# Layer 0's feed-forward in seven block products, with its down-projection a stage of its own, and the state-space tables in two parts

## The chip, the cores and the metric

The kernel runs on one core of a Trainium2 chip. The time is the device time of one execution in microseconds (us). The engines are named as in the profile: PE (TensorE, matrix products, with PEld its weight loads), DVE (VectorE), ACT (ScalarE), POOL (GpSimd) and SP (SyncE, which here issues the DMAs). Each engine works through its own instructions in the order in which the program holds them, and waits where one of them needs another engine's result.

## What is computed

Two layers over 1024 positions of width 1024, all in fp32. Layer 0's mixer is latent attention beside a short gated convolution; layer 1's is a complex-diagonal state-space model. Behind each mixer stands a feed-forward with a convolution of width 3 over the positions; its hidden width is 2816.

```
def conv_ffn(h, w_up, conv_w, w_down):
    up = causal_depthwise_conv(h @ w_up, conv_w)
    gate, val = jnp.split(up, 2, axis=-1)
    return (jax.nn.silu(gate) * val) @ w_down

for layer in range(DEPTH):
    x = x + (mla_shortconv_mixer if layer % 2 == 0 else s5_mixer)(rms_norm(x, ...), ...)
    x = x + conv_ffn(rms_norm(x, ffn_norm[layer]), ffn_w_up[layer], ffn_conv_w[layer], ffn_w_down[layer])
```

The state-space mixer needs, from its small parameters alone, tables for its 64 groups of 16 channels and 64 states: powers of the complex decay, input and output matrices, and a short convolution kernel. They depend on no activation.

## The kernel before

The activations lie transposed in eight tiles xT[0] to xT[7], 128 channels by 1024 positions. Every fp32 product is made of three fp32r products of a high and a low part (`PASSES`: high x high, high x low, low x high), so a product of a 1024-deep unit with 128 columns, `mm_unit` (L175), is 8 x 3 x 2 = 48 matmuls of 128x128 by 128x512. `split_w` (L153, L154) makes the two parts of a weight tile, the high one on ACT, the low one on POOL. Engines run what a scheduler has put in their streams; it orders instructions by the place where the code makes them, as far as their inputs allow.

**Short convolution** (functions up to L290). For m = 0 to 3 there are three units, c, i and b. DVE evicts each from PSUM times the norm (`scaled`, L268: uc, ui, ub), makes the product ut = uc x ui (L282), two steps of the convolution (cv, L285 and L287) and cv x ub (L290); POOL makes the low part cgl (L294). Two down-projections (`down`, L190 matmuls, L193 evictions into xT) follow m = 3. Then comes attention, and behind it the last part of the mixer's down-projection, `down(last_at, w_last, after=bd, skip=3)`.

**Layer 0's feed-forward** (`ffn`). 44 units of 48 matmuls, a gate and a value unit for each of 22 rows; DVE evicts and convolves (L757 to L764), multiplies (L808), and after each pair of rows `down` adds the pair's part of the down-projection, 96 matmuls. Beside it run the state-space tables, in steps: `param_steps` advances the generator `Params.stages` by one, and `ffn` calls it at several places of each row pair.

**The tables** (`Params`). `base` is a chain of some 160 small DVE operations of 128x32 (L868 to L881: exponentials, sine and cosine by polynomials, squarings). `powers` makes the powers of the decay. A `unit(q)`, 16 of them, has three steps: (a) a transpose on PE (pct), and eight small operations (L1042 to L1047, cm and sr); (b) twelve outer products on DVE (L1055 to L1060, tiles z, 128x256 and 128x288); (c) four transposes (pet, L1112) and four small products (pk, L1123) on PE, evictions on ACT and DMAs that store the results in memory. At last 16 `turns(q)`, each a set of outer products of 128x256.

**Layer 1's feed-forward** is done in seven block products: the up-projection's depth of 1024 is cut into two halves of 512, the positions into two halves, and the four block products of a row pair are replaced by seven products of sums of blocks (`Pair`, products "1" to "7", L1648, 12 matmuls each; 22 pairs, 154 products). The sums of the inputs are made in `NormBoundary.second_half`, the sums of weights in `Pair.sums` (POOL, L1628) and `Pair.weights`. The gated rows go to memory (gfd) and the down-projection is a stage of its own behind it, in groups of two and then four rows (`rows`, L1796 the low parts). The inputs xT are stored in memory before they are overwritten and loaded again for the down-projection.

Of the kernel before, what the change touches and what calls it, by code (L numbers as in the profile page):

```python
# [11 lines left out]
F32 = mybir.dt.float32  # L12
# [38 lines left out]
def hybrid_trunk_kernel(ctx: ExitStack, tc: tile.TileContext, xt, gains, mix_w_in, w_uq, w_ukv, q_gain, k_gain,  # L51
# [193 lines left out]

    bases = {"c": CB + CC, "i": CB + 2 * CC, "b": CB}
    with phase("pa") as pA:
# [12 lines left out]
        rx = bd.r  # L260
    pbs = ctx.enter_context(ExitStack())
# [9 lines left out]
    for gr in range(2):  # L271
        gts = []
        for i in range(2):
            m = 2 * gr + i
            if m:
# [3 lines left out]
            ui = scaled(ps_i, "ui")  # L279
            t = pB.tile([P, S + 2], F32, tag="ut", name="ut")  # L280
# [7 lines left out]
                                           op0=ALU.mult, op1=ALU.add)  # L288
            ub = scaled(mm_unit(split_w(ws[2]), xa) if m else first_ps[2], "ub")
# [13 lines left out]
    pbs.close()  # L303
    pR0.close()
# [3 lines left out]
    with phase("pc") as pC, tc.tile_pool(name="psa", bufs=1, space=PSUM, reuse_waits="tile") as pa:  # L308
# [374 lines left out]
        if True:  # L683
# [39 lines left out]
            up_raw = []  # L723
            for n in range(2):
                queue[1].turn()
                up_raw.append(load_up(0, n))
# [5 lines left out]
            up_raw.append(load_up(0, 2))  # L732
            retire(queue.pop(0))()
            add_row()
            up_first = [split_w(r) for r in up_raw]
            tc_order.close()
        last_at = [groups[gr].at for gr in (2, 3)]
        w_last = [w_rows[gr] for gr in (2, 3)]
# [8 lines left out]
    def ffn(layer, bd, rbpool, open_pool, gtile, down_last, background=lambda: None, first=None):  # L747
        dn = ffn_w_down[layer]

        def convolve(ps, m, gate):  # L750
            res = []
            for hf in range(2):
                u = pF.tile([P, HALF + 2], F32, tag="u", bufs=2, name="u")
                if hf == 0:
                    nc.vector.memset(u[:, 0:2], 0.0)
                else:
                    nc.vector.tensor_copy(out=u[:, 0:2], in_=u_last[:, HALF:HALF + 2])  # L757
                u_last = u
                nc.vector.tensor_tensor(out=u[:, 2:HALF + 2], in0=ps[hf], in1=rb[:, HALVES[hf]], op=ALU.mult)  # L759
                c = pF.tile([P, HALF], F32, tag="c", bufs=4, name="c")  # L760
                nc.scalar.activation(c, u[:, 2:HALF + 2], AF.Copy, scale=cwcol(layer, 2, m))  # L761
                nc.vector.scalar_tensor_tensor(out=c, in0=u[:, 1:HALF + 1], scalar=cwcol(layer, 1, m), in1=c,
                                               op0=ALU.mult, op1=ALU.add)
                nc.vector.scalar_tensor_tensor(out=c, in0=u[:, 0:HALF], scalar=cwcol(layer, 0, m), in1=c,  # L764
                                               op0=ALU.mult, op1=ALU.add)
                if gate:
                    nc.scalar.activation(c, c, AF.Silu)
                res.append(c)
            return res

        xs = bd.xs
        prev = None
        loads = [lambda m=m: load_up(layer, m) for m in range(3, 2 * NM)]
        ps, rb = first_units(first or [split_w(load_up(layer, m)) for m in range(3)], xs, bd, rbpool)
        pF = open_pool()
        raw, ready = [loads.pop(0)()], []

        def unit():

            res = ps.pop(0) if ps else mm_unit(ready.pop(0), xs)  # L780
            if len(ps) <= 1:
                if raw:
                    ready.append(split_w(raw.pop(0)))
                if loads:
                    raw.append(loads.pop(0)())
            return res

        def rows_of(gr):
            return [load_row(dn, 2 * gr + i) for i in range(2)]

        for gr in range(NG):
            gts = []
            for i in range(2):
                m = 2 * gr + i
                if gr > 1:
                    background()
                cg = convolve(unit(), m, True)
                if gr:
                    background()
                if gr and i:  # L800
                    rows = [split_w(r) for r in rows]
                cv = convolve(unit(), NM + m, False)
                if gr and not i:
                    rows = rows_of(gr - 1)
                gh, gl = gtile(pF, "gh"), gtile(pF, "gl")
                for hf in range(2):
                    cols = HALVES[hf]
                    nc.vector.tensor_tensor(out=cv[hf], in0=cv[hf], in1=cg[hf], op=ALU.mult)  # L808
                    nc.scalar.activation(gh[:, cols], cv[hf], AF.Copy)  # L809
                    nc.gpsimd.tensor_tensor(out=gl[:, cols], in0=cv[hf], in1=gh[:, cols].bitcast(F32),  # L810
                                            op=ALU.subtract)
# [1061 lines left out]
```

## Time and profile before

| | us |
|---|---|
| median of three runs (lowest, highest) | 2345.22 (2342.04, 2348.31) |
| the profiled execution, and its span | 2344.66, 2342.9 |
| short convolution, to the last matmul of its down-projections | 49.4 to 196.38 |
| attention | 201.76 to 513.86 |
| last part of the mixer's down-projection | 513.86 to 530.91 |
| layer 0's feed-forward with the tables | 530.91 to 1293.39 |
| state-space mixer and its output | 1293.39 to 1628.08 |
| layer 1's products | 1644.60 to 2096.77 |
| layer 1's down-projection | 2096.77 to 2337.94 |

The dates come from the chain of work that ended last: starting at the last instruction, it names at each step what released it, or the instruction before it on its engine. The stretch view gives, for the time between two dates, how long each engine was busy and with how many instructions, the granted TensorE clock (1.00 is full speed) and the mean busy share of the DMA engines. TensorE was busy for 2248.5 us of the span.

### The profile page before, as it was taken

To read this page: it belongs to the slowest core of one execution; us is meant where nothing else is said; L and a number is where in the kernel's file an instruction comes from. 1 tells how busy PE (TensorE), PEld (TensorE's weight loads), DVE (VectorE), ACT (ScalarE), POOL (GpSimd) and SP (SyncE) were. 2 spreads that over 40 slices of the span, in tenths; PEclk is the share of its full clock that TensorE was granted. 3 is DMA by queue.
4 is the path that set the end of the run, shared out by engine and by line. 5 is a ranking of instruction groups with operands and counts; after the bars stand their busy time and mean duration, and the time that the engine had idled before them with its cause. 6 is when DMAs were issued, how large, how long until landed. Compare 5 with 4: busy or idle time off the path is not lost.

```text
span 2342.9 us, 29810 instructions
## 1 busy us (share of the span) xinstructions
PE 2248.5 (96%) x11228; PEld 1867.9 (80%) x11228; DVE 1614.7 (69%) x2650; ACT 851.3 (36%) x1446; POOL 767.0 (33%) x575
## 2 busy tenths in 40 slices
PE   7999899999999999999999988999789999999999
PEld 6888888888788878888888877788568888878887
DVE  6344677787978778879777487323888888876542
ACT  4112566664232333332223255312444444443110
POOL 4322454435233222232224344431043333324220
PEclk9999999999999999999999998999999999999999
DMA  4112000012122221223332288521132222245301
GB/s 155 45 38 57 1 10 10 10 46 72 29 66 62 82 68 49 76 80 92 101 102 63 93 223 242 171 72 41 54 110 93 82 81 81 81 153 181 125 10 72
DMA packets 227152, 192.04 MB, mean 82 GB/s; under 512 B 25472, under 2 KB 202944, under 8 KB 227008
## 3 DMA queue, kind: packets, MB, share of 16 engines
q1 hardware_dynamic: 227008, 190.14, 26.9%
q8 instruction: 88, 1.44, 0.2%
q14 instruction: 56, 0.46, 0.1%
HBM read 148.22 MB, written 46.07 MB: 83 GB/s over the span
## 4 chain that ended last, share of the span: by engine, by line
PE 79%; DVE 11%; issue 3%; DMA 3%; ACT 3%; POOL 1%; SPq 0%; DVEq 0%; POOLq 0%; ACTq 0%
PE pu L175 31%; PE pd L190 22%; PE pc L1648 4%; PE pb L1648 4%; PE pa L1648 4%; PE pd L1648 2%; PE pu L1554 1%; PE pss L586 1%; PE po L634 1%; PE pckv L378 1%; PE pq L446 1%; PE ptp L615 1%; DVE xT L1696 1%; PE pcq L378 1%; PE pda L644 1%
## 5 line engine op out<-in xcount | busy, mean ns | idle before, releaser
L154 POOL TENSOR_TENSOR wl<-raw,wh 128x1024 fp32r<-128x1024 f32 (+2 forms) x115 | 289.1, 2515 | 487.3 <-ACT wh L153 242.3
L193 DVE TENSOR_TENSOR xT<-pd,xT 128x512 f32<-128x512 f32 x320 | 204.3, 682 | 160.4 <-PE pd L190 159.8
L153 ACT ACTIVATE wh<-raw 128x1024 fp32r<-128x1024 f32 (+2 forms) x117 | 122.4, 1051 | 305.8 <-PE pu L175 212.6
L175 PE MATMUL pu<-f_h,wh 128*128 128x512 f32 x704 | 219.4, 393 | 0.0
L175 PE MATMUL pu<-f_l,wh 128*128 128x512 f32 x704 | 217.2, 390 | 0.0
L175 PE MATMUL pu<-f_h,wl 128*128 128x512 f32 x704 | 216.7, 389 | 0.0
L175 PEld LDWEIGHTS pu<-f_l,wh 128*128 128x128 f32 x704 | 132.1, 188 | 27.9
L175 PEld LDWEIGHTS pu<-f_h,wl 128*128 128x128 f32 x704 | 132.1, 188 | 27.9
L175 PEld LDWEIGHTS pu<-f_h,wh 128*128 128x128 f32 x704 | 130.7, 188 | 28.7 <-issue 1.7
L810 POOL TENSOR_TENSOR gl<-c,gh 128x512 fp32r<-128x512 f32 x44 | 61.4, 1415 | 247.0 <-ACT gh L809 247.0
L1696 DVE SCALAR_TENSOR_TENSOR xT<-u,vec,xT 128x1024 f32<-128x1024 f32 x84 | 111.1, 1330 | 13.3 <-ACT xT L1694 12.6
L759 DVE TENSOR_TENSOR u<-pu,f_rb 128x512 f32<-128x512 f32 x88 | 56.8, 685 | 89.9 <-PE pu L175 87.9
L190 PE MATMUL pd<-gh,wh 128*128 128x512 f32 x352 | 113.5, 403 | 5.4 <-DVE u L759 2.9
L190 PE MATMUL pd<-gh,dwh 128*128 128x512 f32 x352 | 108.8, 390 | 2.5 <-DVE xT L193 1.5
L190 PE MATMUL pd<-gl,wh 128*128 128x512 f32 x352 | 110.4, 395 | 0.0
L190 PE MATMUL pd<-gh,wl 128*128 128x512 f32 x352 | 110.0, 394 | 0.0
L190 PE MATMUL pd<-gh,dwl 128*128 128x512 f32 x352 | 108.5, 389 | 0.0
L190 PE MATMUL pd<-gl,dwh 128*128 128x512 f32 x352 | 108.4, 389 | 0.0
L1796 POOL TENSOR_TENSOR dwl<-raw,dwh 128x1024 fp32r<-128x1024 f32 x20 | 60.8, 3066 | 112.5 <-PE pd L190 84.3
L761 ACT ACTIVATE c<-u,vec 128x512 f32<-128x512 f32 x88 | 59.9, 717 | 69.5 <-DVE u L759 69.1
L190 PEld LDWEIGHTS pd<-gh,wh 128*128 128x128 f32 x352 | 65.8, 191 | 22.6 <-DVE xT L193 4.0
L190 PEld LDWEIGHTS pd<-gh,dwh 128*128 128x128 f32 x352 | 66.1, 188 | 16.9 <-DVE xT L193 1.9
(569 smaller groups left out, 5790.6 us busy)
## 6 DMA issues: line engine op xcount, KB each, us to landing
raw<-in_ffn_w_up_dram SPq DMA_DIRECT2D x50, 512.0 KB, 3.8
raw<-in_ffn_w_down_dram SPq DMA_DIRECT2D x42, 512.0 KB, 4.4
xT<-in_ffn_w_up_dram SPq DMA_DIRECT2D x40, 512.0 KB, 3.6
gfd<-xT SPq DMA_DIRECT2D x21, 512.0 KB, 2.6
raw<-gfd SPq DMA_DIRECT2D x20, 512.0 KB, 4.0
raw<-in_w_glu_dram SPq DMA_DIRECT2D x16, 512.0 KB, 4.0
raw<-in_mix_w_in_dram SPq DMA_DIRECT2D x14, 512.0 KB, 3.9
xT<-in_xt_dram SPq DMA_DIRECT2D x8, 512.0 KB, 7.6
```

Source lines behind the costliest of these rows:

```text
L153: nc.scalar.activation(h[:, 0:n], raw[:, 0:n], AF.Copy)
L154: eng.tensor_tensor(out=l[:, 0:n], in0=raw[:, 0:n], in1=h[:, 0:n].bitcast(F32), op=ALU.subtract)
L175: nc.tensor.matmul(ps[hf], lhsT=w[wi][:, P * k:P * k + P], rhs=xs[k][xi][:, HALVES[hf]], start=(k == 0 and wi == 0 and xi == 0), stop=(k = ...
L190: nc.tensor.matmul(ps[hf], lhsT=ws[i][wi][:, P * f:P * f + P], rhs=gts[i][xi][:, HALVES[hf]], start=(i == first and wi == 0 and xi == 0), ...
L193: nc.vector.tensor_tensor(out=xT[f][:, HALVES[hf]], in0=ps[hf], in1=xT[f][:, HALVES[hf]], op=ALU.add)
L378: nc.tensor.matmul(ps[:, HALF * j:HALF * j + n], lhsT=xa[k][xi][:, P * (2 * p + j):P * (2 * p + j) + P], rhs=w[k // kw][wi][:, n * (k % kw ...
L759: nc.vector.tensor_tensor(out=u[:, 2:HALF + 2], in0=ps[hf], in1=rb[:, HALVES[hf]], op=ALU.mult)
L761: nc.scalar.activation(c, u[:, 2:HALF + 2], AF.Copy, scale=cwcol(layer, 2, m))
L810: nc.gpsimd.tensor_tensor(out=gl[:, cols], in0=cv[hf], in1=gh[:, cols].bitcast(F32), op=ALU.subtract)
L1648: nc.tensor.matmul(ps, lhsT=w[:, HALF * wi + P * k:HALF * wi + P * k + P], rhs=x.at(xi, k), start=(start and k == 0 and wi == 0 and xi == ...
L1696: nc.vector.scalar_tensor_tensor(out=c, in0=u[:, w:S + w], scalar=cwcol(self.layer, w, m), in1=c, op0=ALU.mult, op1=ALU.add)
L1796: eng.tensor_tensor(out=l, in0=raw, in1=h.bitcast(F32), op=ALU.subtract)
```

## The change

Layer 0's feed-forward is done as layer 1's is. The code of layer 1 becomes the class `FeedForward(layer)` with the methods `add`, `sums`, `spread`, `first_half`, `second_half`, `up`, `rows` and `begin_down`, and `Pair(ff, m)`; layer 1 uses it with unchanged steps. From the state-space stage on every engine holds the same instructions in the same order as before. The last part of the mixer's down-projection is made half by half of the positions; the first half's norm is begun during the second half.

The class `Params` moves ahead of the first stage and its generator is cut in two. `first_part` has base, powers and units 0 to 7, is driven by calls in the short convolution (two steps a call, three calls for each m) and by every second block of its two down-projections, and then stores what the rest needs (`keep`, 128x1314) in memory. `second_part` loads it again, has units 8 to 15 and the turns, and is driven by one step for each of the eight blocks f of each group of layer 0's new down-projection. The loads and splits of the first three units of layer 0's up-projection at the end of attention are gone.

```diff
@@ short convolution, for each m = 2 * gr + i
             ui = scaled(ps_i, "ui")
+            background(2)
             t = pB.tile([P, S + 2], F32, tag="ut", name="ut")
...
+            background(2)
             ub = scaled(mm_unit(split_w(ws[2]), xa) if m else first_ps[2], "ub")
...
             gts.append((gh, gl))
+            background(2)
...
-            down(*held_down)
-            down(gts, wr)
+            down(*held_down, after=lambda f: background(f % 2))
+            down(gts, wr, after=lambda f: background(f % 2))
@@ Params
+        def first_part(self):
+            yield from self.base()
...
+            yield from self.units(0, SPLIT)
+            nc.sync.dma_start(out=kpd, in_=self.keep)
+            yield
+        def second_part(self):
+            nc.sync.dma_start(out=self.keep, in_=kpd)
+            yield from self.units(SPLIT, NP // 2)
...
@@ behind attention
-    down(last_at, w_last, after=bd, skip=3)
+    ff = FeedForward(0)
+    for hf in range(2):
+        for f in range(KT):
+            ps = psum("pd")
...
+            if hf and f == 2:
+                ff.sums(0)
...
+            ff.add(f, hf)
+            if hf and f == 5:
+                ff.spread(0)
+                ff.first_half()
...
-    ffn(0, bd, pF0, open_params, lambda pool, name: pool.tile([P, S], F32R, tag="gt", bufs=6, name=name),
-        close_params, background=param_steps, first=up_first)
+    ff.up()
+    groups_d = [(0, 2)] + [(r, r + 4) for r in range(2, 18, 4)] + [(18, 20), (20, 22)]
+    ready_d = ff.begin_down(groups_d[0])
+    params.open("b")
+    stages = params.run(params.second_part())
+    for n in range(len(groups_d) - 1):
+        gts, ws = ready_d
+        last = n == len(groups_d) - 2
+        ready_d = ff.rows(*groups_d[n + 1], ff.d_tile if last else atile)
+        down(gts, ws, after=lambda f: background())
+    for _ in stages:
+        pass
```

The order of the instructions, first on PE in the short convolution. In the names, a_h and a_l are the parts of the normalised input, with the number of the tile; wh and wl are a unit's weights. Before, at the border between the second unit of m = 1 (i, up to a_h_171) and the third (b, from a_h_124):

```order
L175 MATMUL pu<-a_h_171,wh 128x512 x2
L175 MATMUL pu<-a_l_172,wh 128x512 x2
L175 MATMUL pu<-a_h_171,wl 128x512 x2
L175 MATMUL pu<-a_h_124,wh 128x512 x2
L175 MATMUL pu<-a_l_125,wh 128x512 x2
L175 MATMUL pu<-a_h_124,wl 128x512 x2
```

After, at the same border (i ends with a_h_178, b begins with a_h_131; L544 is pet, L555 pk, z_784 and z_785 the two tensors of unit 0):

```order
L175 MATMUL pu<-a_h_178,wh 128x512 x2
L175 MATMUL pu<-a_l_179,wh 128x512 x2
L175 MATMUL pu<-a_h_178,wl 128x512 x2
L518 MATMUL pct<-ident,ct 128x64
L544 MATMUL pet<-ident,z_784 128x2x64
L555 MATMUL pk<-z_784,bd_804 32x128
L175 MATMUL pu<-a_h_131,wh 128x512 x2
L175 MATMUL pu<-a_l_132,wh 128x512 x2
L175 MATMUL pu<-a_h_131,wl 128x512 x2
L175 MATMUL pu<-a_h_136,wh 128x512 x2
```

Unit 0's transposes and products now stand between two units of the short convolution, and three more transposes a few matmuls into the next.

On DVE at the same place. Before, the evictions and products of m = 1:

```order
L268 TENSOR_TENSOR uc<-pu,a_rb 128x512 x2
L268 TENSOR_TENSOR ui<-pu,a_rb 128x512 x2
L282 TENSOR_TENSOR ut<-uc,ui 128x1024
L285 SCALAR_TENSOR_TENSOR cv<-ut,vec,cv 128x1024
L287 SCALAR_TENSOR_TENSOR cv<-ut,vec,cv 128x1024
L268 TENSOR_TENSOR ub<-pu,a_rb 128x512 x2
```

After, the end of the base chain (L304 to L317, scr and keepa), unit 0's outer products (L487 to L492, z_784) and the eviction of i (L674, ui):

```order
L479 TENSOR_TENSOR sr_787<-cm_796,cm_797 128x32
L304 TENSOR_TENSOR scr<-keepa 128x32 x2
L317 SCALAR_TENSOR_TENSOR keepa<-keepa 128x32
L487 TENSOR_TENSOR z_784<-sr_786,keepa 128x2x128
L304 TENSOR_TENSOR keepa<-scr 128x32
L304 TENSOR_TENSOR scr<-keepa 128x32
L674 TENSOR_TENSOR ui<-pu,a_rb 128x512
L304 TENSOR_TENSOR scr<-keepa 128x32
L674 TENSOR_TENSOR ui<-pu,a_rb 128x512
```

The eviction of i, which stood directly behind that of c, now stands behind the base chain, and the convolution's steps are mixed with unit 0's outer products.

On PE in layer 0's feed-forward, around the transposes of a unit. Before, a unit with a whole product of 48 matmuls ahead of it (f_h and f_l are the parts of the normalised input):

```order
L175 MATMUL pu<-f_h_5882,wh 128x512 x2
L175 MATMUL pu<-f_l_5883,wh 128x512 x2
L175 MATMUL pu<-f_h_5882,wl 128x512 x2
L1112 MATMUL pet<-ident,z_7531 128x2x64
L1112 MATMUL pet<-ident,z_7532 128x2x64
L1112 MATMUL pet<-ident,z_7531 128x2x64
L1112 MATMUL pet<-ident,z_7532 128x2x64
L1123 MATMUL pk<-z_7531,bd_7551 32x128
L1123 MATMUL pk<-z_7532,bd_7552 32x128
L1123 MATMUL pk<-z_7531,bd_7551 32x128
L1123 MATMUL pk<-z_7532,bd_7552 32x128
L175 MATMUL pu<-f_h_5735,wh 128x512 x2
```

After, at the beginning of the new down-projection: the third block of its first group (gh, gl the gated rows, dwh, dwl the weights), then unit 8, the first of the second part:

```order
L190 MATMUL pd<-gh,dwh 128x512 x2
L190 MATMUL pd<-gl,dwh 128x512 x2
L190 MATMUL pd<-gh,dwl 128x512 x2
L544 MATMUL pet<-ident,z_10078 128x2x64
L544 MATMUL pet<-ident,z_10079 128x2x64
L544 MATMUL pet<-ident,z_10078 128x2x64
L544 MATMUL pet<-ident,z_10079 128x2x64
L555 MATMUL pk<-z_10078,bd_10098 32x128
L555 MATMUL pk<-z_10079,bd_10099 32x128
L555 MATMUL pk<-z_10078,bd_10098 32x128
L555 MATMUL pk<-z_10079,bd_10099 32x128
L190 MATMUL pd<-gh,dwh 128x512 x2
```

The transposes stood behind a whole product of the up-projection, and stand now behind the third block of the down-projection's first group.

## Rows read from the trace of the kernel before

**Rows 1.** Busy by stretch: length, PE, PEld, DVE, ACT, POOL, clock, DMA share, GB/s.

```profile
49.40:198.80 149.40, 148.76 (x652) 121.83 (x651) 69.12 (x73) 23.00 (x22) 41.86 (x20) 1.00 0.16 44
530.90:1293.40 762.50, 756.33 (x3402) 612.81 (x3401) 603.99 (x1249) 239.55 (x444) 247.81 (x121) 1.00 0.26 72
1644.60:2096.80 452.20, 433.55 (x1858) 350.76 (x1858) 380.96 (x434) 202.87 (x286) 133.95 (x123) 0.98 0.27 90
...
700.00:1290.00 590.00, 589.74 (x2676) 478.15 (x2675) 466.88 (x870) 179.80 (x353) 181.14 (x88) 1.00 0.28 78
```

**Rows 2.** The chain that ended last: start, us, what.

```profile
513.86 17.05 PE pd L190 x74
...
1293.39 21.81 PE pu L175 x96
...
1622.50 5.58 PE pu L1554 x24
1644.60 9.61 PE pa L1648 x34
...
1766.41 2.72 PE pd L1648 x12
...
2109.41 228.53 PE pd L190 x1006
```

**Rows 3.** DVE in order of time, short convolution: start, us, instruction, idle before.

```profile
52.17 1.23 DVE L282 TENSOR_TENSOR ut<-uc,ui 128x1024 f32<-128x1024 f32 x1
...
76.60 1.29 DVE L268 TENSOR_TENSOR ui<-pu,a_rb 128x512 f32<-128x512 f32 x2 [9.59 <-PE pu L175]
77.92 2.48 DVE L282 TENSOR_TENSOR ut<-uc,ui 128x1024 f32<-128x1024 f32 x1
81.69 2.06 DVE L285 SCALAR_TENSOR_TENSOR cv<-ut,vec,cv 128x1024 f32<-128x1024 f32 x1 [1.28 <-ACT cv L284]
83.79 1.28 DVE L287 SCALAR_TENSOR_TENSOR cv<-ut,vec,cv 128x1024 f32<-128x1024 f32 x1
```

**Rows 4.** Groups of instructions, 600:1310 (DVE), 590:1310 (PE): busy, mean ns.

```profile
L1055 DVE TENSOR_TENSOR z<-sr,ap 128x256 f32<-128x256 f32 (+1 forms) x32 | 18.8, 588 | 0.0
...
L1057 DVE TENSOR_TENSOR z<-sr,ap 128x256 f32<-128x256 f32 (+1 forms) x32 | 15.8, 494 | 1.2 <-DMA cpd<-z 1.1
...
L1123 PE MATMUL pk<-z,bd 128*32 128x128 f32 x128 | 10.2, 279 | 0.0
L1112 PE MATMUL pet<-ident,z 128*128 128x128 f32 x64 | 9.6, 272 | 0.0
```

**Rows 5.** DVE in order of time: the last pair's product in layer 1.

```profile
2107.54 1.21 DVE L1705 TENSOR_TENSOR cv<-cv 128x1024 f32<-128x1024 f32 x1
```

**Rows 6.** DVE in order of time, base chain of the tables.

```profile
595.07 0.28 DVE L964 COPY hold<-pbase 128x32 f32<-128x32 f32 x2
...
601.47 2.40 DVE L868 TENSOR_TENSOR scr<-scr 128x32 f32<-128x32 f32 x1
```

**Rows 7.** Busy time by stretch, convolution before i's eviction and base chain.

```profile
53.40:76.60 23.20, 23.20 (x104) 19.22 (x103) 7.78 (x7) 4.52 (x5) 4.90 (x3) 1.00 0.26 69
...
595.00:632.00 37.00, 36.31 (x160) 29.66 (x158) 36.36 (x187) 9.20 (x17) 9.80 (x5) 1.00 0.07 19
```

**Rows 8.** Groups of DVE instructions, 595:632: other work, longest and shortest of five.

```profile
L764 DVE SCALAR_TENSOR_TENSOR c<-u,vec,c 128x512 f32<-128x512 f32 x5 | 3.6, 743 | 0.0
...
L808 DVE TENSOR_TENSOR c<-c 128x512 f32<-128x512 f32 x2 | 1.3, 682 | 0.0
```

**Rows 9.** PE in order of time, around a wait in layer 0's feed-forward.

```profile
630.69 0.62 PE L190 MATMUL pd<-gh,wl 128*128 128x512 f32 x2
...
634.25 1.40 PE L190 MATMUL pd<-gh,wh 128*128 128x512 f32 x2 [2.94 <-DVE u L759]
```

**Rows 10.** POOL in order of time, in both places.

```profile
601.43 4.91 POOL L154 TENSOR_TENSOR wl<-raw,wh 128x1024 fp32r<-128x1024 f32 x2 [9.05 <-issue]
...
76.93 5.75 POOL L154 TENSOR_TENSOR wl<-raw,wh 128x1024 fp32r<-128x1024 f32 x2 [12.15 <-issue]
```

More of the change, by code (lines that the diff above doesn't have):

```diff
@@ L260, in hybrid_trunk_kernel, with background @@
         rx = bd.r
+    params.open("a")
+    stages = params.run(params.first_part())
+    def background(n=1):
+        for _ in range(n):
+            next(stages, None)
     pbs = ctx.enter_context(ExitStack())
@@ L744, in dump @@
             nc.sync.dma_start(out=dbg[name][P * f:P * f + P, :], in_=xT[f])
[L747 to L762, printed above, removed]
-                                               op0=ALU.mult, op1=ALU.add)
[L764 to L811, printed above, removed]
-                gts.append((gh, gl))
-            if gr == NG - 1:
-                last_rows = rows_of(gr)
-            if gr:
-                down(prev, rows, after=lambda f: None if f % 2 else background())
-            prev = gts
-        down_last(prev, [split_w(r) for r in last_rows])
@@ new lines, in hybrid_trunk_kernel @@
+    last_rows, last_w = [groups[gr].at for gr in (2, 3)], [w_rows[gr] for gr in (2, 3)]
+    ff = FeedForward(0)
+    for hf in range(2):
+        for f in range(KT):
+            ps = psum("pd")
+            first = 1 if f < 3 else 0
+            for i in range(first, 2):
+                for wi, xi in PASSES:
+                    nc.tensor.matmul(ps, lhsT=last_w[i][wi][:, P * f:P * f + P], rhs=last_rows[i][xi][:, HALVES[hf]],
+                                     start=(i == first and wi == 0 and xi == 0), stop=(i == 1 and wi == 1))
+            if hf and f == 2:
+                ff.sums(0)
+            x = xT[f][:, HALVES[hf]]
+            nc.vector.tensor_tensor(out=x, in0=ps, in1=x, op=ALU.add)
+            ff.add(f, hf)
+            if hf and f == 5:
+                ff.spread(0)
+                ff.first_half()
@@ L1222, in hybrid_trunk_kernel @@
+    for _ in stages:
+        pass
+    params.close()
+    ps0 = ctx.enter_context(ExitStack())
+    bd = Boundary(ps0.enter_context(phase("pfb1")), "ssm", 0, "s5")
+    down(*ready_d, after=bd)
     if "x2" in dbg:
         dump("x2")
-        ps0.close()
-        pf.close()
         return
-    bd = bd_box[0]
     prb1 = ctx.enter_context(ExitStack())
@@ L1708, in hybrid_trunk_kernel @@
-    pairs = [Pair(1, m) for m in range(FIRST + 1)]
-    early = pairs[0:FIRST]
-    for p in pairs:
-        p.weights("12")
-    pps.close()
-    pbk = pps.enter_context(tc.tile_pool(name="psu", bufs=1, space=PSUM, reuse_waits="tile"))
-    def bank_tile(bank, name):
-        return pbk.tile([P, HALF], F32, tag=f"ps{bank}", bufs={"a": 3, "b": 2, "c": 2, "d": 1}[bank], name=name)
-    xb = {"1": nb.b11, "2": nb.b21}
-    for p in pairs:
-        p.product("1", "a", True)
-    nb.sums(1)
-    pbt.close()
@@ L1723, in hybrid_trunk_kernel @@
-    puc = ctx.enter_context(ExitStack())
-    pU = puc.enter_context(phase("pu"))
-    for p in pairs:
-        p.keep()
-    for p in early:
-        p.sums()
-        p.weights("56")
-    blocks = nb.second_half()
-    pairs[0].product("2", "a", False)
-    nb.spread(1)
-    xb["5"] = next(blocks)
-    for p in pairs[1:]:
-        p.product("2", "a", False)
-    xb["6"] = next(blocks)
-    for p in early:
-        p.weights("74")
-    pairs[0].evict()
-    for j in "56":
-        for p in early:
-            p.run(j)
@@ L1743, in hybrid_trunk_kernel @@
-    for p in early:
-        p.weights("3")
-    for j in "74":
-        xb[j] = next(blocks)
-        early[0].run(j)
-        early[1].product(j, "b" if j == "7" else "d", j == "4")
-        if j == "7":
-            early[1].add(early[1].p1, "b", early[1].p1)
-    pairs[FIRST].load(False)
-    pairs[FIRST].sums()
-    pairs[FIRST].weights("65743")
-    xb["3"] = next(blocks)
-    early[0].run("3")
-    early[0].finish()
-    for j in "65":
-        pairs[FIRST].run(j)
-    early[1].evict()
-    early[1].lower("c", HALF)
```

1271 lines of the change are left out of this document (656 added, 615 removed).

## The prediction, made before the result was known

> **What bounds the kernel now.** I read first how busy each engine is in the stretches that the change touches. TensorE is busy 148.76 of 149.40 us in the short-convolution stage, 756.33 of 762.50 in layer 0's feed-forward, 433.55 of 452.20 in layer 1's products [rows 1]: all three are bound by matmuls. VectorE is the engine behind it: 69.12 us of 149.40 in the convolution stage, 603.99 of 762.50 in the feed-forward, where it also works out the state-space tables. Then the chain of work that ended last, for dates and for the price of a matmul: twelve in 2.72 us, 0.2267 us each [rows 2]. It gives the parts to be compared: the mixer's last down-projection begins at 513.86, the feed-forward behind it ends at 1293.39; layer 1's is entered at 1628.08 (1622.50 + 5.58), its first product starts at 1644.60 and its last matmul ends at 2337.94 (2109.41 + 228.53).
>
> The sum is made against the profiled execution, 2344.66 us with a span of 2342.9, half a microsecond under the median of the runs, so I carry the result over unchanged. A measurement of this kernel tells apart about 0.3%, 7 us.
>
> **Layer 0's feed-forward.** It had 44 x 48 up matmuls and gets 154 products of 12, that is 1848: 264 fewer, 59.9 us at 0.2267. What it really takes is read from layer 1, where the same code runs: 693.3 us from first product to end [rows 2]. Ahead of it come the mixer's down-projection half by half, 78 matmuls or 17.7 us. Its first half no longer waits for the lows of the last two attention rows, so I start it 2.7 us (twelve matmuls) sooner, at 511.1; the squares' sum and the spreading of the norm take an estimated 2.6. Between the spread and the first product VectorE has eight normalisations and eight splits of 128x512 to do, at 0.65 us or more each (the evictions in [rows 3], pairs of the same size, take 1.29), 10 to 13 us, with one spare block of twelve matmuls, 2.7 us, over it; I let TensorE idle 10.6. Layer 1's entry idled 16.5 [rows 2]. Stores of the block inputs queue on SP ahead of the weights of the first pairs: 2.5 us. The second half of the tables is still TensorE work: the two large table lines are 10.2 + 9.6 us for 16 units [rows 4], 1.24 a unit, 9.9 for eight. The end is then 511.1 + 17.7 + 2.6 + 10.6 + 693.3 + 2.5 + 9.9 = 1247.7 instead of 1293.4: **46 us sooner**, if the tables fit under the down-projection.
>
> They don't at its start. A table unit is 12 outer products on VectorE, by six lines from 588 ns down to 494 ns a piece [rows 4], 6.5 us, with the small ones about 8. The first group has two rows, 96 matmuls or 21.8 us, and the program puts 2.67 units into it: 21 us, plus 16 evictions of 0.65 and some splits of the next group, nearly 38 us of VectorE. The transposes of unit 8 stand on TensorE right behind the third block of the group, about 8 us after its start; but the tables come back from memory by a load that stands on SP behind the store of the last pair, whose last operation in layer 1 came at 2107.54 [rows 5], 11 us after the down-projection had begun (2096.8). Load, eight small operations and twelve outer products put the transposes 13 to 17 us late, and the rest of the group some 5 more. In the four-row groups a block is 24 matmuls, 5.4 us: three blocks, 16 us, for a unit of 8 and six evictions of 0.65; that fits. I take **20 us** (8 where the load is early and evictions interleave well, 35 where every unit up to the second group lags). Net for this part: -26.
>
> **The convolution stage.** Here 38 us of small base work and eight units come under a stage in which TensorE has no slack [rows 1]. What decides is that TensorE's own order is fixed: behind the second product of m = 1 (i) stand unit 0's transposes and products, and only then the third (b). Before, i's eviction came at 76.60 and b followed without a gap [rows 1, 3]. Now VectorE must first go through the base chain and unit 0. That chain took from 595.07 to 632 before [rows 6, 7], VectorE busy 36.36 of 37.0 [rows 7]; five lines of other work in it, from L764 with 3.6 us to L808 with 1.3 [rows 8], make 11.9, which leaves 25 for the chain. It can start when the first ut is done (52.17 + 1.23 = 53.4), next to 7.78 us of the stage's own work up to i's eviction [rows 3, 7]: i is evicted at 53.4 + 25 + 7.8 = 86, ten late. Behind the eviction (1.3) come ut, two cv, six outer products and the rest of the squarings, 2.5 + 2.1 + 1.3 + 3.2 + 1.5, so unit 0 is there at about 98; TensorE has waited since 77.3: **20 us** (12 if GpSimd stops none of it, 27 if it stops it at each of its splits). Fifteen matmuls (3.4 us) further on, transposes want the unit's second tensor, some 6 us of VectorE work behind the first: 3 us.
>
> In m = 2 and m = 3 two steps are run in one call, so again a unit's transposes follow its outer products with only i in front. i's eviction, ut and both cv took from 76.60 to 85.07 in the same place [rows 3]; with eight of the outer products beside them some 11 us, less 1.5 of table work of the unit before: 9.5 each, **19 us** (12 to 28). The other units have a whole product or four blocks of down-projection for cover; they cost their matmuls, 8 x 1.24, of which some lie in the waits: 7 (4 to 10). [...] On SP the column loads of m = 3 now stand behind unit 0's stores, but two products, 22 us, lie between them and their use: nothing. The attention that follows is only shifted. Sum: 20 + 3 + 19 + 7 + 5 = **+54 us** (31 to 75).
>
> **GpSimd in it.** One effect needs its own look. In the base chain a 128x32 operation took 2.40 us at 601.47, up to the end of a 128x1024 subtraction that GpSimd had begun at 601.43 (two in 4.91) [rows 6, 10]. [...] In the convolution stage GpSimd has such splits at 76.93, 5.75 us for two [rows 10], just where the first chain would run. My 25 us hold the four that fell into the chain before; if all fall in, the first wait is 7 longer and each later one 5.
>
> **The rivals.** (1) *The tables hide after all; faster.* Mechanism: VectorE runs the 160 small operations at the 0.1 us that two interleaved chains can reach (18 us for the chain instead of 25), ut and cv go undisturbed, and group 0's load comes early. First wait 12, later ones 4 each, matmuls 4, clock 3: 27; feed-forward -46 + 8 = -38. Net -11, **2334**. It decides at a convolution-stage cost under about 26 us. For it: TensorE was busy 589.74 of 590 us under the same units before [rows 1]. Against: there each unit had a whole feed-forward block between its outer products and its transposes; here it has none. (2) *Between:* stage cost 35, group 0 at 12: **2346**. (3) *GpSimd stops all of it.* First wait 27, later ones 14 each, with 15 of lesser costs: 70; group 0 at 30: net 54, **2399**. For it: the row at 601.47. Against: most splits of the stage stand at unit borders, and GpSimd waits for VectorE itself. (4) *Layer 1's time doesn't carry over.* At layer 0's entry 4 MB of stores and the first pairs' weights share SP's queue; if the first weights come 15 us late as well, 2372 + 15 = **2387**. (5) *The change doesn't do what it says:* the products are there in the order of the instructions, as is the split of the tables, so I give it nothing.
>
> **How the numbers follow.** Forecast: 2344.7 - 26 + 54 = 2372.7, **2372 us**, with a chance of 0.52. Rival 1: 0.13; 2: 0.08; 3: 0.14; 4: 0.13. Faster is rival 1 alone, 0.13; the same is rival 2, 0.08; slower the rest, 0.79. The forecast's own bounds are 2372 - 23 - 12 and 2372 + 21 + 15, that is 2337 to 2408 if everything went one way; the range reaches to rivals 1 and 3: 2334 to 2402.
>
> **What would show it right or wrong.** Right: after the changed kernel's second product of m = 1 TensorE waits 12 to 27 us for VectorE, in m = 2 and 3 some 10 us each in the same place, and the stage's last matmul comes 45 to 65 us after 196.4; layer 0's feed-forward then takes 25 to 30 us less than before, with a wait of 13 to 17 us in the first group of its down-projection. Wrong in sign, if the stage ends before 222, or if the base chain was worked through before i's eviction at 77. Wrong in size, if layer 0's products differ from layer 1's 693.3 us by more than the 20 of group 0, or if SP's queue delays the third pair of column loads in the convolution stage.

## The result, and the profile after

The changed kernel takes 2402.56 us (median of four runs, 2400.39 to 2404.02) against 2345.87 us for the kernel before beside it: a ratio of 1.0242, 95% interval 1.0225 to 1.026. It is slower by 57 us where the forecast was 27. The direction was right; the time lies 0.6 us above the upper end of the range. The profiled execution took 2404.02 us, its span is 2402.2 us.

First the busy time by stretch, as in [rows 1], with the kernel's new borders (length, then PE, PEld, DVE, ACT and POOL, the granted TensorE clock, DMA share, GB/s): the convolution stage, the entry into layer 0's products, these products, layer 0's down-projection, the state-space mixer, layer 1.

```profile
49.40:255.40 206.00, 167.90 (x749) 132.43 (x748) 148.29 (x436) 42.41 (x113) 38.54 (x19) 0.90 0.22 58
573.20:608.00 34.80, 21.80 (x98) 17.14 (x96) 28.10 (x44) 17.33 (x29) 15.17 (x12) 0.87 0.57 186
608.00:1057.00 449.00, 433.98 (x1854) 352.61 (x1854) 382.15 (x433) 203.55 (x286) 133.75 (x124) 0.98 0.28 90
1057.00:1346.90 289.90, 257.00 (x1160) 207.00 (x1161) 220.40 (x431) 72.42 (x140) 68.49 (x25) 0.95 0.46 131
1346.90:1685.90 339.00, 310.72 (x1517) 261.04 (x1516) 158.24 (x212) 120.57 (x158) 130.59 (x71) 0.95 0.49 142
1685.90:2397.30 711.40, 687.27 (x2965) 558.07 (x2963) 518.24 (x575) 253.00 (x340) 194.58 (x143) 0.99 0.28 94
```

In the convolution stage TensorE was busy for all but 0.6 us [rows 1] and now idles 38 of 206 us; in the down-projection it idles 33 of 290. The products take 433.98 us of TensorE in 449.0, layer 1's 433.55 in 452.20 [rows 1]: that part carried over. The chain of work that ended last gives the dates (start, us, what), as [rows 2] did before:

```profile
97.12 5.41 PE pu L175 x15
...
146.21 12.28 PE pu L175 x48
...
192.27 12.88 PE pu L175 x47
...
251.00 4.34 PE pd L190 x18
...
606.55 1.44 PE f_st L1221 x6
607.99 5.17 PE pa L1447 x12
...
1323.91 22.95 PE pd L190 x94
1346.87 21.76 PE pu L175 x96
...
1680.35 5.58 PE pu L1765 x24
...
2379.80 17.47 PE pd L190 x77
```

Laid against the forecast's own borders, the kernel's end comes 31 us later than the sum said (2397.3 instead of 2366.2, the old end of 2337.9 and the 28.3 of the sum):

| part | forecast | measured | difference |
|---|---|---|---|
| end of the convolution stage | 196.4 + 54 | 255.4 | +5 |
| from there to the last down-projection of the mixer | 314.7 | 317.8 | +3 |
| from there to the first product | 30.9 | 34.8 | +4 |
| products of layer 0 (452.2 + 2.5 for weights behind stores) | 454.7 | 449.0 | -6 |
| its down-projection (241.1 + 9.9 + 20) | 271.0 | 289.9 | +19 |
| state-space mixer and its output | 334.7 | 339.1 | +4 |
| layer 1 | 709.9 | 711.3 | +1.5 |

The dates 196.4 and 255.4 are where the chain leaves the convolution stage, in both kernels six matmuls (1.4 us) ahead of its last one. More than half of the miss is the down-projection. TensorE's waits in it, by what ended them (total, times, longest):

```profile
PE pct L518 <- DMA ct<-in_c_im_dram: 20.6, 1, 20.6
PE pd L190 <- ACT gh L1363: 10.5, 1, 10.5
PE pd L190 <- DVE xT L193: 1.7, 1, 1.7
```

The first is at the beginning, the second at the last group of rows. Neither ends with an outer product. SP's own instructions (SPq, the issuing of DMAs) in order of time, at the first place and at the second:

```profile
1068.81 0.32 SPq L1504 DMA_DIRECT2D gfd<-cv  x1
...
1073.32 0.42 SPq L624 DMA_DIRECT2D keepb<-kpd  x1
...
1075.63 0.60 SPq L508 DMA_DIRECT2D ct<-in_c_im_dram  x1
```

```profile
1310.28 5.20 SPq L590 DMA_DIRECT2D csd<-wt  x8
...
1316.17 0.65 SPq L1374 DMA_DIRECT2D raw<-gfd  x1
```

The tables' reload (keepb) and the inputs of unit 8 stand behind the store of the last pair (gfd<-cv, 1068.81), as forecast. TensorE, though, meets the unit's first transpose (pct, of the loaded ct) already behind the first block, not the third, and stops there:

```profile
1056.97 0.50 PE L190 MATMUL pd<-gh,dwh 128*128 128x512 f32 x1 [1.01 <-DVE u L1452]
...
1080.40 0.34 PE L518 MATMUL pct<-ident,ct 64*128 64x64 f32 x1 [20.64 <-DMA ct<-in_c_im_dram]
...
1322.60 1.22 PE L190 MATMUL pd<-gh,dwh 128*128 128x512 f32 x2 [10.46 <-ACT gh L1363]
```

At the end, the load of a gated row of the last group (raw<-gfd, 1316.17) is issued behind eight stores of a turn (csd<-wt); 6.4 us later TensorE gets the row. What such stores wait for, the longest entry of SP's own waits in this stage (total, times, longest):

```profile
SPq L590 <- DVE wt L491: 20.4, 3, 10.4
```

The convolution stage, TensorE's waits and the first of them, then VectorE in order of time:

```profile
PE pet L544 <- DVE z L491: 25.4, 3, 15.5
PE pk L555 <- DVE z L491: 10.7, 3, 3.8
PE pk L555 <- DVE z L492: 2.1, 1, 2.1
```

```profile
92.23 0.48 PE L544 MATMUL pet<-ident,z 128*128 128x128 f32 x1 [15.55 <-DVE z L491]
96.52 0.61 PE L555 MATMUL pk<-z,bd 128*32 128x128 f32 x2 [3.81 <-DVE z L491]
```

```profile
76.80 2.21 DVE L475 TENSOR_TENSOR cm<-keepa 128x32 f32<-128x32 f32 x1
...
85.86 0.68 DVE L674 TENSOR_TENSOR ui<-pu,a_rb 128x512 f32<-128x512 f32 x1
...
87.16 2.28 DVE L304 TENSOR_TENSOR scr<-scr 128x32 f32<-128x32 f32 x1
```

i's eviction, at 76.60 before [rows 3] and forecast for 86, is at 85.86. The two small operations above stood still beside GpSimd's splits: 2.34 us each, begun at 76.62 and 87.05.

### The profile page after: what moved, and what is told of

Read it like the earlier page. It is cut to its first block, busy times and chain, and to the rows that moved or that the text cites. A ratio compares the mean times of both kernels' runs of the same rounds, so it can differ in the third digit from the quotient of the medians.

```text
span 2402.2 us, 29692 instructions
## 1 busy us (share of the span) xinstructions
PE 2210.8 (92%) x10964; PEld 1830.8 (76%) x10964; DVE 1714.2 (71%) x2660; ACT 914.0 (38%) x1538; POOL 724.2 (30%) x612
## 4 chain that ended last, share of the span: by engine, by line
PE 72%; DVE 16%; DMA 4%; issue 3%; ACT 3%; POOL 2%; SPq 1%; DVEq 0%; POOLq 0%; ACTq 0%
PE pd L190 20%; PE pu L175 10%; PE pb L1447 9%; PE pc L1447 9%; PE pa L1447 8%; PE pd L1447 4%; DVE w L1437 1%; DMA cs<-csd 1%; PE pu L1765 1%; DVE xT L1494 1%; PE pss L998 1%; PE po L1046 1%; PE pckv L790 1%; PE pq L858 1%; DVE xT L1243 1%
## 5 line engine op out<-in xcount | busy, mean ns | idle before, releaser
L190 PE MATMUL pd<-gh,dwh 128*128 128x512 f32 x704 | 221.1, 395 | 15.5 <-ACT gh L1363 10.5
L190 PE MATMUL pd<-gh,dwl 128*128 128x512 f32 x704 | 217.6, 391 | 0.7 <-POOL dwl L1364 0.7
L154 POOL TENSOR_TENSOR wl<-raw,wh 128x1024 fp32r<-128x1024 f32 (+2 forms) x49 | 121.8, 2486 | 281.8 <-ACT wh L153 194.1
L190 PEld LDWEIGHTS pd<-gh,dwl 128*128 128x128 f32 x704 | 132.6, 189 | 28.9 <-POOL dwl L1364 1.1
L190 PEld LDWEIGHTS pd<-gl,dwh 128*128 128x128 f32 x704 | 132.5, 189 | 28.8 <-DVE gl L1364 1.2
L1437 DVE TENSOR_TENSOR w<-xT,w 128x512 fp32r<-128x512 f32 x116 | 136.4, 1176 | 0.0
L1447 PE MATMUL pc<-b22h,w 128*128 128x512 f32 x352 | 119.5, 400 | 12.4 <-DVE u L1452 9.1
L1447 PE MATMUL pb<-t3h,w 128*128 128x512 f32 x352 | 119.4, 402 | 6.6 <-ACT t3h L1164 6.6
L1447 PE MATMUL pa<-b11h,w 128*128 128x512 f32 x352 | 118.7, 400 | 4.6 <-ACT w L1436 4.3
L1447 PE MATMUL pb<-t2h,w 128*128 128x512 f32 x352 | 118.0, 395 | 0.7 <-ACT w L1436 0.5
L1447 PE MATMUL pd<-t4h,w 128*128 128x512 f32 x352 | 117.2, 393 | 1.1 <-ACT t4h L1164 1.1
L1447 PE MATMUL pc<-t1h,w 128*128 128x512 f32 x352 | 116.0, 391 | 0.5 <-ACT t1h L1164 0.4
```

The costliest lines, as they stand in the source:

```text
L154: eng.tensor_tensor(out=l[:, 0:n], in0=raw[:, 0:n], in1=h[:, 0:n].bitcast(F32), op=ALU.subtract)
L190: nc.tensor.matmul(ps[hf], lhsT=ws[i][wi][:, P * f:P * f + P], rhs=gts[i][xi][:, HALVES[hf]], start=(i == first and wi == 0 and xi == 0), ...
L1437: nc.vector.tensor_tensor(out=t[:, HALF:S], in0=self.src[j], in1=t[:, 0:HALF].bitcast(F32), op=ALU.subtract)
L1447: nc.tensor.matmul(ps, lhsT=w[:, HALF * wi + P * k:HALF * wi + P * k + P], rhs=x.at(xi, k), start=(start and k == 0 and wi == 0 and xi == ...
```

## The experiments

Each kernel is the changed one with the edit shown, and an edit that several of them have is shown where it stands first. Left-out lines are marked with three dots.

**One call later in the convolution.** A unit's step on TensorE (c) is issued one call after its outer products, and the first of the three calls for each m stands behind c, so that a whole product lies between.

```diff
@@ unit(q)
-            yield
+            if not self.lag:
+                yield
@@ first_part
-            yield from self.units(0, SPLIT)
+            yield from self.lagged(0, SPLIT)
@@ lagged: for each unit
+                if k:
+                    next(steps[k - 1])
+                    self.flush()
+                next(step)
+                yield
@@ short convolution, for each m: behind c, ahead of b and behind the gating
-            background(2)
+            background(1 if m else 2)
...
-            down(gts, wr, after=lambda f: background(f % 2))
+            down(gts, wr, after=lambda f: background(f % 4 == 3))
```

> The changed kernel with one thing moved: in the convolution stage a unit's transposes and products (step c) are issued one call later than its outer products (steps a and b), and the calls stand behind c, i and b of each m instead of twice behind i, so a whole product of 48 matmuls lies between. The work is the same. Theory A (the 59 us of the stage are mostly matmuls waiting in order behind table transposes, 38 us of waits and 5 us of slow clock behind them): the waits fall to under 8 us, some 15 us of table matmuls stay, the stage ends at 207 to 223 instead of 255 and the time is 2352 to 2375. Rival B (VectorE itself is short in this stage, with GpSimd's splits stopping it): the waits only move to the evictions, the stage ends behind 245 and the time is 2392 to 2405.

2369.64 us, 1.011 of the kernel before (1.0093 to 1.0127), 33 less than the changed kernel. The stage ends at 224.4 instead of 255.4 (expected 207 to 223); what TensorE still waits there:

```profile
PE pk L557 <- DVE z L492: 6.0, 1, 6.0
PE pet L546 <- DVE z L492: 4.5, 1, 4.5
PE pet L546 <- DVE z L493: 1.9, 1, 1.9
```

12.4 us instead of 38.2; I had expected under 8. All three waits stand at unit 0, behind the base chain (between 93 and 110 us), and those of m = 2 and m = 3 are gone. So two thirds of the waits came from where the steps stand, not from the amount of table work: that is the same in both.

**The second part's first step earlier.** The loads of unit 8 are issued ahead of the first group, and no table step stands in it.

```diff
@@ second_part
+            self.loaded = self.load(SPLIT)
+            yield
-            yield from self.units(SPLIT, NP // 2)
+            yield from self.units(SPLIT, NP // 2, self.loaded)
@@ layer 0's down-projection
+    background()
...
-        down(gts, ws, after=lambda f: background())
+        down(gts, ws, after=lambda f: background(0 if n == 0 else 1 + (f % 4 == 1)))
```

> The changed kernel with one thing moved in layer 0's down-projection: the loads of the second part of the tables are issued at its start, but no table step runs in the first group of two rows; the steps follow from the second group on, 10 in each group of 8 blocks. Theory A (TensorE waited 20.6 us there for one load of unit 8 that is queued behind the loads of the handover): that wait, the 1.7 us behind it and some 2 us of slow clock go, the 10.5 us before the last group stay: 2372 to 2390. Rival B (the handover's own loads of rows and weights are late as well): TensorE waits for gated rows instead and the time is 2393 to 2403.

2398.4 us, 1.0236 (1.0219 to 1.0252): 4 less. That is above the 2372 to 2390 of theory A and in the rival's range, but not by the rival's mechanism: the second wait below is for outer products. The wait for ct is gone, but:

```profile
PE pd L190 <- ACT gh L1365: 9.4, 1, 9.4
PE pk L555 <- DVE z L491: 9.4, 1, 9.4
```

The last group's wait stayed, and a new one came in the second group, where now two steps fall into some calls. GpSimd and VectorE at that place, in order of time:

```profile
1089.91 12.36 POOL L1366 TENSOR_TENSOR dwl<-raw,dwh 128x1024 fp32r<-128x1024 f32 x5 [11.43 <-ACT dwh L1365]
```

```profile
1090.00 2.63 DVE L490 TENSOR_TENSOR om<-sr,keepb 128x256 f32<-128x256 f32 x1
1092.55 2.62 DVE L491 TENSOR_TENSOR z<-z,om 128x256 f32<-128x256 f32 x1
1095.08 2.63 DVE L492 TENSOR_TENSOR z<-z,om 128x256 f32<-128x256 f32 x1
1097.64 2.37 DVE L476 TENSOR_TENSOR cm<-bt,keepb 128x32 f32<-128x32 f32 x1
```

Five splits in a row on GpSimd, and in the first four of them only one VectorE operation each, which took 2.4 to 2.6 us. Just ahead an operation of 128x256 took 0.41 us and one of 128x32 0.18. That these 10 us are the wait of 9.4 is argued from the rows; no run tried it by itself.

**Both edits together.**

> The moves of the two runs before together. If the two costs are independent, as theory A has it, their gains add up: 2328 to 2358, about 2340, which is the saving of the block products with what the table matmuls cost. If one shift of the program only hands the loss on (loads of layer 0 that come due sooner), less than their sum: 2360 to 2380.

2363.52 us (1.0082, 1.0067 to 1.0097): only 6 less than the first edit alone, and in the range of the rival expectation. The two measured gains do add up (33 and 4 for 39 together); what was missing was the gain of the second edit. The same two waits are there, 9.4 and 9.0 us.

**Eleven units in the first part** (`SPLIT = 11` on top, and one step a block from the second group on), so that the second part has three units less.

> As the run before with 11 units instead of 8 in the first part, three more in the two down-projections of the convolution stage, and one step a block from the second group of layer 0's down-projection on, so that the turns end earlier. Theory A (the wait of 10.5 us before the last group comes from table stores that the last rows' loads are queued behind): that wait shrinks, the table matmuls cost the same in either place: 2318 to 2348, faster than the kernel before. Rival (VectorE is full in those down-projections, 4 units of 8 us and 21 us of evictions against 43.5 us of matmuls): the stage ends 10 us later than in the run before and nothing is gained over it.

2359.77 us (1.0067, 1.0047 to 1.0087), 4 less than without it and above the 2318 to 2348 that I expected. The rival's longer convolution stage did not come either: its last matmul ends at 227.2, with eight units at 229.0. The wait in the second group fell to 2.2 us, the last one is the largest left:

```profile
PE pd L190 <- ACT gh L1381: 12.0, 1, 12.0
```

```profile
1268.29 2.84 SPq L592 DMA_DIRECT2D csd<-wt  x4
...
1271.87 0.40 SPq L1392 DMA_DIRECT2D raw<-gfd  x1
```

Less work for VectorE had not moved it; the row still came out of the queue behind the turns' stores. That led to the next edit.

**The turns' stores on ScalarE's queue**, alone, on the changed kernel.

```diff
@@ turns(q)
-                        nc.sync.dma_start(out=dst, in_=wt[j][64 * g:64 * g + 64])
+                        nc.scalar.dma_start(out=dst, in_=wt[j][64 * g:64 * g + 64])
```

> The changed kernel with one thing altered: the stores of the turns (csd) are issued by ScalarE's DMA queue instead of SP's. Theory A (TensorE's wait of 10.5 us before the last group of layer 0's down-projection is the last rows' load queued on SP behind stores that wait for VectorE's turns): that wait goes to under 2 us, with 1 to 2 us of slow clock behind it: 2389 to 2394. Rival B (the load waits for its buffer or for the memory queues): the wait stays and the time is 2400 to 2404.

2395.18 us (1.0211, 1.0191 to 1.0231), 7.4 less. The work is the same, only the queue of the stores differs, and the wait for the last group's row, 10.5 us, is gone from the stage; this one stands first now, and none of the others is over 1.8 us:

```profile
PE pct L518 <- DMA ct<-in_c_im_dram: 21.6, 1, 21.6
```

This shows the cause: the load waited on SP behind stores that waited for VectorE. The time lies 1 us above the 2389 to 2394 of theory A.

**All of it:** the later call, the earlier loads, eleven units and the stores' queue, and the units of the convolution one call later still.

```diff
             yield
-            yield from self.units(0, SPLIT)
+            yield
+            yield from self.lagged(0, SPLIT)
```

> All moves together: tables lagged by one product in the convolution stage and begun one call later still, 11 units in the first part, no table step in the first group of the down-projection, turn stores on ScalarE's queue. Theory A: the convolution stage waits under 4 us for tables and ends about 20 us behind 196.4 (11 units of table matmuls and base), the down-projection has no wait over 3 us: 2328 to 2342, faster than the kernel before. If instead VectorE is the bound where the waits are gone (conv stage's down-projections, second part's turns): 2345 to 2356.

2340.73 us, median of ten runs, against 2345.18 for the kernel before (19 runs): 0.9982, 0.9971 to 0.9994. Layer 0's feed-forward ends at 1283.00, where it ended at 1293.39 before. TensorE's waits in the two stages, convolution and down-projection:

```profile
PE pet L546 <- DVE z L493: 7.5, 1, 7.5
```

```profile
PE pd L190 <- DVE xT L193: 3.7, 4, 1.4
PE pk L557 <- DVE z L492: 2.2, 1, 2.2
```

The 7.5 us are more than the 4 that I expected in the convolution; two waits more, of 1.4 and 1.3 us, stand behind the stage's last matmul, where the last unit's steps run on until attention begins at 228. This kernel takes 19 us less than the one with eleven units. Layer 0's feed-forward gives 17 of them: from its first product to its end it takes 707.1 us instead of 723.7. How much of that is the queue and how much anything else was not taken apart.

The seven products are no loss, then, once the tables' TensorE steps and DMAs stand where nobody waits: 62 us of the changed kernel came from where and on which queue its steps stand, since the arithmetic is the same. Against the kernel before, 4 us is all that is left of the gain: the convolution stage, which now has table work in it, still ends 24 us later than before (221.6 instead of 197.7, both to the last matmul).

**GpSimd for six of the low parts.** On top of that, the first weights' low parts in the entry of both layers' feed-forward are made on GpSimd instead of VectorE, to shorten the 34.8 us.

```diff
-                p.weights("12")
+                p.weights("12", nc.gpsimd)
...
-                nc.vector.tensor_tensor(out=t[:, HALF:S], in0=self.src[j], in1=t[:, 0:HALF].bitcast(F32),
+                eng.tensor_tensor(out=t[:, HALF:S], in0=self.src[j], in1=t[:, 0:HALF].bitcast(F32),
```

> The run before with the low parts of the first six weight blocks at the entry of either feed-forward made by GpSimd instead of VectorE. If VectorE's queue is what TensorE waits 11.6 us for there (normalising, splits, then weights), each entry is 2 to 4 us shorter: 4 to 8 us below the run before. If GpSimd's subtractions stop VectorE's operations on SBUF while they run, as in the base chain of the tables, nothing is gained or it is up to 5 us slower.

2342.87 us (ten runs; 0.9991, 0.9981 to 1.0001): nothing gained, and the 2 us more are within the two intervals. Layer 0's entry took 34.7 us with and without the edit, and its wait (the squares' sum f_st on VectorE's squares, 11.6 us) is the same in the changed kernel and in both of these: the low parts are not what TensorE waits for there. What would shorten it stays open.

**The bare down-projection.** No table step in it; the second part is done in one piece ahead of the last group of rows that the loop leaves.

```diff
-        down(gts, ws, after=lambda f: background())
+        down(gts, ws)
```

> The changed kernel with no table step inside layer 0's down-projection: the whole second part is done behind the fifth group, ahead of the sixth, so nothing is left out. Theory A (the 290 us of this stage are the bare 241 us of layer 1's stage and 49 us that the second part adds: 33 us of waits, the rest table matmuls): the groups up to the drain run with no wait above 3 us, a block of 24 matmuls takes 5.4 to 5.6 us, and the stage without the drain takes 241 to 246 us; the drain itself, half of the tables with VectorE alone at work, takes 55 to 85 us, so the kernel is at 2400 to 2435 us, not faster than the changed one. Theory B (the stage is slower in layer 0 by itself, by its loads of gated rows and weights): waits of 5 us or more for a DMA or an operand stay in the bare groups, and the stage without the drain takes over 252 us.

2476.03 us (1.0563, 1.051 to 1.0616), above my 2400 to 2435. The bare groups held what was expected: 960 matmuls from 1053.8 to 1275.8, 222.0 us where 0.2267 each makes 217.6, and in the chain one unbroken piece:

```profile
1084.84 190.93 PE pd L190 x841
```

With 96 more matmuls that is 244 us, so layer 0's stage costs within 3 us what layer 1's does (241). In the changed kernel it takes 290: the tables add 46, of which 33 are waits. What I had too low is the second part in series: its units end 58 us later, at 1333.9, and the turns hold up the state-space stage behind them, whose norm TensorE awaits:

```profile
PE s_st L225 <- POOL s_sq L219: 51.8, 1, 51.8
```

**The bare convolution stage.** The same for the first part.

```diff
-            background(2)
...
-            down(*held_down, after=lambda f: background(f % 2))
-            down(gts, wr, after=lambda f: background(f % 2))
+            down(*held_down)
+            down(gts, wr)
```

> The changed kernel with no table step inside the short convolution: the first part is done behind the convolution's down-projections, ahead of attention, so nothing is left out. Theory A (the stage itself is unchanged and its 59 us are what the first part adds): the last matmul of the down-projections comes at 196 to 199 us as before, and the first part then takes 75 to 100 us in series, which means that the convolution hid only a third or less of it; kernel 2415 to 2445 us. Theory B (part of the 59 us comes from something else in the stage, as more loads or another order of splits): the down-projections end after 203 us although no table step stands in the stage.

2426.79 us (1.0353, 1.0299 to 1.0408). The stage's last matmul ends at 195.3:

```profile
179.93 15.35 PE pd L190 x67
```

Before it ended at 197.7, which is the 196.4 and the six matmuls that the chain leaves out, and in the changed kernel at 256.7. So the stage without table steps is no slower than before, and the table steps cost all of its loss, 61 us. In series the first part takes until 278, 83 us, so the convolution hid some 22 of them. Busy time of the first ten microseconds and of ten later ones:

```profile
200.00:210.00 10.00, 0.00 (x0) 0.00 (x0) 9.69 (x87) 0.23 (x1) 0.00 (x0) 0.50 0.22 64
...
240.00:250.00 10.00, 5.25 (x21) 2.65 (x23) 8.30 (x29) 2.69 (x12) 0.00 (x0) 0.50 0.35 82
```

With nothing beside it the base chain is VectorE's alone (87 operations in 10 us), and takes some 20 us, from 196.5 to unit 0's first outer product at 217.27; the units then follow every 7.0 us (their stores go out at 231.4, 238.4, 245.4).

## Why the prediction was right, and where it was wrong

**Convolution stage: right in its waits, too low in its matmuls.** Forecast 54, measured 59.0. The first two waits are 15.55 and 3.81, 19.4 together (forecast 20 and 3), i's eviction came at 85.86 (86), the waits of m = 2 and m = 3 are 9.0 and 7.7 (9.5 each), a last one 2.1: 38.2 in all for 42. Too low was the rest: 12 for table matmuls and clock, measured 20.9 (TensorE busy 167.9 instead of 147.0). The last term of the sum, 5 for the clock, is one that no run shows as it stands; the trace of before has two matmuls in 1.40 us instead of 0.62 behind a wait of 2.94 [rows 9]. What the changed kernel showed in its place: 15 matmuls in 5.41 us, 48 in 12.28 and 47 in 12.88, at 0.2267 each 2.0, 1.4 and 2.2 us too long, 5.6 together, each behind one of the waits, at a granted clock of 0.50 (90 to 100, 144 to 148 and 190 to 196 us). Without these 5.6, some 15 are left for the table matmuls, forecast at 7. The 1.24 us a unit left out the transposes pct, 0.27 to 0.28 us each in this stage, and I had let part of the rest lie in the waits; but they stand behind the waits, partly at the granted clock of 0.50 (four pet in 1.24 us at 140.11, in 0.60 at 180.57). The bare stage and the later call show the mechanism: without the steps there is no wait, and with the same steps one product later two thirds of the waits are gone.

**GpSimd: between.** It does stop VectorE, but in the first chain only three of the small operations met a split (at 62.57, 76.62 and 87.05), some 2.3 us each, of which my 25 us held four. A fourth split, at 55.00, stopped a step of the convolution itself, cv, for 3.48 us instead of 1.27. So the forecast date of i's eviction came out with about the delays that it held, and rival 3 didn't come about here. VectorE's evictions from PSUM were not stopped: in the changed kernel's down-projection two took 1.29 us beside the splits, as just ahead of them (1101.46) and in [rows 3], and an operation of 128x32 after them took 2.38. GpSimd's five splits ran there from 1104.16 to 1116.61.

```profile
1104.62 1.29 DVE L193 TENSOR_TENSOR xT<-pd,xT 128x512 f32<-128x512 f32 x2
...
1107.10 2.38 DVE L474 TENSOR_TENSOR cm<-bt,keepb 128x32 f32<-128x32 f32 x1
```

**Layer 0's products: right.** 449.0 against 452.2 from layer 1; the 2.5 us for weights behind stores didn't show. Of the 46 us that the seven products were to give, little is missing besides the tables' waits: 4 us at the entry, 3 ahead of it and 3 in the bare down-projection, against 6 gained in the products.

**The step that failed: the 20 us for tables under the down-projection.** The wait that I described, at unit 8 by SP's order, is there and has the size (20.6 us for a forecast 20). But the waiting instruction is another: pct, two blocks sooner, for a load and not for the outer products; I had looked at the order from the third block on. And a second place was not in the sum at all: at the other end of the stage the turns' stores stand on the queue that loads the last group's rows, 10.5 us. I had costed what table work does to VectorE and TensorE, and of its DMAs only those of the beginning; the stores of the turns, which share SP with the loads of the stage itself, I didn't follow. Moving these stores alone gave 7.4 us back. With 1.7 for an eviction the waits are 32.8 us where the term was 20; table matmuls and clock took 16, forecast 9.9 for the matmuls alone. Together 48.8 instead of 29.9.

**The smaller ones.** The entry took 34.8 us, forecast 30.9. TensorE idled 13.0 us in it, where I had 10.6 for the normalisation; 11.6 of them are one wait for the second half's squares, which VectorE makes behind the first half's normalisation. And it was busy 21.8 us, forecast 20.3, at a granted clock of 0.87 in the stretch. Rival 4, weights late by SP's queue, didn't come about: the wait there ends with VectorE. The state-space mixer took 4.4 us more with the same instructions in the same order (TensorE busy 310.72 for 310.23 before, so it is idling). Its longest wait is for a reload of the tables (9.9 us, where before it was one of 9.4 for other data). The variants with nothing put ahead of this stage lie between 1.6 us less and 6.7 more than before, so the cause of the 4.4 is open. So are the 1.5 us in layer 1 and the 3 in attention.

**Sign and chances.** Slower held. Nearest to 2402.56 is rival 3's 2399, but not by its mechanism: it had a first wait of 27, later ones of 14 each and 30 in group 0, and 19.4, 9.0, 7.7 and 20.6 were measured. The whole of layer 0's part, forecast at a net gain of 26, gave 5.5: its end is 53.5 us late behind a convolution that is 59.0 late. What I underrated is how many of the small terms lie on one side: six of the seven parts came out above the forecast, and a range that reaches 30 us up from the likeliest had no room for one unforeseen wait beside them.

## What to carry to other kernels

Background work that is cut into steps brings three things to its new place: time on its own engine, instructions in the order of the engine that is the bound, and DMAs on a queue. Follow each to its end, the last step of the generator as closely as the first: here stores that waited for VectorE, one of them 10.4 us, held up the load behind them on SP, and TensorE waited 10.5 us for the row; and a step on the bounding engine needs other work between it and what it reads, as a whole product here took away two thirds of the waits (38.2 us to 12.4). The work does not become free by that: the stage that took it over still ends 24 us later. But 62 us here hung on where the steps stood and which queue the stores took.

## What the runs showed of the hardware

In the changed kernel an operation of 128x32 on VectorE took 0.18 us, and in two interleaved chains one was begun every 0.10 to 0.12 us (79.13 to 80.08); beside GpSimd's splits the same operation took 2.2 to 2.4 us, and one of 128x256 2.6 instead of 0.41 (the second experiment), in a run of splits about one operation for each split. With the turns' stores issued by ScalarE instead of SyncE, TensorE's wait of 10.5 us for the last group's row was gone, and none of its waits in that stage ended with ScalarE. TensorE's granted clock was 0.50 from 90 to 100 us of the changed kernel, at the end of its wait and just behind it, and 15 large matmuls behind that wait took 5.41 us instead of the 3.40 that 0.2267 each makes.
